# A decoder step on one core: another order of the mixers' work for the scheduler, with the retention projections 1.6 times further apart

## The chip, the cores and the metric

The kernel runs on one core of one Trainium2 chip. The metric is the device time of one execution in microseconds, as the median of several runs. The engines are TensorE (PE in the profile; PEld is its weight loading), VectorE (DVE), ScalarE (ACT), GpSimd (POOL) and SyncE (SP), whose queue issues most of the DMAs.

## The reference

One inference step of a two-layer decoder over 512 prompt rows and 64 sample rows, 576 together, 1024 wide. Layer 0 has two mixers side by side: RWKV-7 time mixing (mixer A, 8 heads of 64) and retention (mixer B, 8 heads of 64). One input projection feeds both, and one output projection takes both. Cut to the core:

```python
def ab_mixer(x, ...):
    proj = x @ w_in
    pa, pb = proj[..., :A_PROJ], proj[..., A_PROJ:]
    ya, shift1, wkv1 = rwkv7_mixer(pa, ...)     # S = S*w + sa*(kk*a) + v*k, o = S r, step by step
    q, kr, vr, gate = jnp.split(pb, 4, axis=-1)
    ob, ret1 = retention(rope(q), rope(kr), vr, ret0, log_gamma)
    yb = silu(gate) * head_norm(ob, gn_g, gn_b)
    return concatenate([ya, yb]) @ w_out, shift1, wkv1, ret1

for l in range(2):
    y = ab_mixer(x) if l % 2 == 0 else conv_mixer(x)
    x = layer_norm(ALPHA * x + y)
    x = layer_norm(ALPHA * x + squared_relu_mlp(x))
```

The states at the end of both mixers and of the convolution are outputs too.

## The kernel before

Everything is held transposed: a tile has 128 columns of the model on its partitions and the 576 rows along it, in two halves of 288 (`GN`). A weight is loaded in fp32 and cut into a high and a low part of type fp32r (ScalarE casts, VectorE or GpSimd subtracts), and each product is three matmuls (`mm3`, lines 152 to 154): high by high, high by low, low by high. A tile of a projection is 8 x 2 x 3 = 48 matmuls of 288 columns.

The mixers of layer 0 come first, up to some 497 us; the rest (the trunk: layer norms, MLPs, the convolution layer) follows and isn't touched. In the mixers the heads go in pairs, p = 0 to 3, for either mixer. `build` (from line 1346) writes them as twelve generators, which are numbered in the order of the call of `drive` in line 1493:

- 0, `projs`: 28 projection tiles in the order of `SEQ`. n = 0 to 2 are mixer A's k, r, v of pair 0, 3 to 5 of pair 1, 6 to 9 retention's q, k, v, gate of pair 0, 10 to 12 mixer A's of pair 2, 13 retention's q of pair 1, 14 to 16 mixer A's of pair 3, and 17 to 27 the eleven tiles left for retention pairs 1, 2 and 3. Most are spilled to DRAM (`spill`, `spillA`) through the one tile stg. At the end the pools of the projections are closed, the tiles x are loaded into the room that this gives (line 1427), and 'proj' is done.
- 1 `pres` and 2 `stages`: the preparation of mixer A's pairs, one after the other (`pre`, `stage`; L700 is the first matmul of a stage).
- 3 to 6, `back(p)`: `inverse` (L791 and L803), `scan` (L847 to L875), `ya`. The scan has a chain of seven steps: a matmul into the PSUM tile ch (L863), then an addition on VectorE (L865). Then come the products into the PSUM tile po.
- 7 `samples`, the sample rows' state.
- 8 `ret_fronts` (loads, rope, transposes), 9 `ret_backs((0, 2))`, 10 `ret_backs((1, 3))`: the retention (`ret_back`, `hnorm`). `ret_fronts` starts when the last stage is done, and waits for 'proj' before pairs 2 and 3. `ret_back` accumulates in ch for pairs 0 and 2, in po for pairs 1 and 3 (the tile is called rpo there).
- 11 `wout`: the output projection in three parts (`WP`, line 1342): tiles y0 to y2 when 'proj' and 'ya2' are done, y3 to y5 when 'ya3', 'ret0' and 'ret1' are, y6 when 'ret2' is. Its sums in PSUM are called wa; L1306 and L1307 cut its weights, L1336 and L1338 add to x. The last tile, y7, is multiplied at the start of the trunk.

ch, po and other tiles exist once, so who takes one first holds up the next. A generator yields a number (how long its step counts), a condition, or a lock that is taken (1, name) or given back (-1, name).

What sets the order: `drive` advances the generators one step at a time and gives each step a number, `tc.cur_priority`. The scheduler that lays out each engine's instructions takes the ready one of the lowest number. In the kernel before, steps and numbers are a table of 424 pairs (generator, number), `SCHEDULE`, which `drive` reads out:

```python
    base = tc.cur_priority
    for c, p in SCHEDULE:
        tc.cur_priority = base + p
        next(gens[c], None)
```

Conditions and locks that the generators yield have no effect there; the table stands for them. In it generator 0 goes from 100000 to 120421, by 735 a tile, and the largest number is 132485, of `wout`. The engines' queues are in order, so the layout is fixed when the program is built.

Of the kernel before, what the change touches and what calls it, by code (L numbers as in the profile page):

```python
# [1222 lines left out]
def post(o):  # L1223
# [9 lines left out]
            c(sh[1:][None]), c(wk(o['swkv'])), c(rt(o['sret'])), c(cv[1:][None]))  # L1233


SCHEDULE = (
# [33 lines left out]
)  # L1270


def drive(tc, *gens):

    base = tc.cur_priority
    for c, p in SCHEDULE:
        tc.cur_priority = base + p
        next(gens[c], None)
    tc.cur_priority = base + max(p for _, p in SCHEDULE) + 10000


CFG = {(n, g): dict(ds=() if n else tuple(range(8)), dq=() if n else tuple(range(8)), sv=(7,), qv=(7,), pg=(1, 2, 3, 4, 5, 6, 7), mulv=(0, 3, 6), affv=()) for n in range(4) for g in range(2)}
# [63 lines left out]
def build(tc, i, o, coff):  # L1346
    nc = tc.nc
    T = Trunk(tc, i['w'], ahead=2)
    with ExitStack() as es:
# [9 lines left out]
        with ExitStack() as s1:  # L1359
# [48 lines left out]
            def projs():  # L1408
                for n, (kind, p, j) in enumerate(SEQ):
                    if kind == 'A':  # L1410
                        M.proj_A(p, j, 2 + n)
                    elif kind == 'S':
                        M.spillA(p, j, 2 + n)
                    else:
                        M.spill(2 + n, 'qkvg'[j] + str(p))
                    yield
                nc.sync.dma_start(o['shift'], M.sho)
                sx.close()
                xp = pool('xp', 1, sr, side='right')
                T.x = [xp.tile([P, NT], F32, name=f'x{k}') for k in range(KT)]  # L1420
                yr = pool('yr', 1, sq, side='right')
                M.y[6:8] = [yr.tile([P, NT], F32, name=f'y{k}') for k in (6, 7)]
                W.y[6:8] = M.y[6:8]
                W.wq = pool('wq', 1, sq, side='right')
                W.acc = pool('wacc', 2, se, space=PSUM)
                for k in range(KT):
                    nc.gpsimd.dma_start(T.x[k], i['x'][:, k])
                M.done.append('proj')
# [282 lines left out]
```

## Time and profile before

| | us |
|---|---|
| median of 3 runs | 1575.98 |
| lowest and highest run | 1573.06, 1576.76 |
| profiled execution, its own time | 1570.47 |
| its span, first to last instruction | 1568.7 |
| PE busy in it | 1476.0 (94%) |
| mean granted clock of PE | 0.968 |

Busy times are those of the profiled execution, counted from the start of its span. A matmul counts as busy from its start to its modelled end, and matmuls overlap, so a stretch in which PE is busy throughout may hold more or fewer of them. The clock is a share of full speed.

### The profile page before, as it was taken

To read this page: it belongs to the slowest core of one execution; us is meant where nothing else is said; L and a number is where in the kernel's file an instruction comes from. 1 tells how busy PE (TensorE), PEld (TensorE's weight loads), DVE (VectorE), ACT (ScalarE), POOL (GpSimd) and SP (SyncE) were. 2 spreads that over 40 slices of the span, in tenths; PEclk is the share of its full clock that TensorE was granted. 3 is DMA by queue.
4 is the path that set the end of the run, shared out by engine and by line. 5 is a ranking of instruction groups with operands and counts; after the bars stand their busy time and mean duration, and the time that the engine had idled before them with its cause. 6 is when DMAs were issued, how large, how long until landed. Compare 5 with 4: busy or idle time off the path is not lost.

```text
span 1568.7 us, 29898 instructions
## 1 busy us (share of the span) xinstructions
PE 1476.0 (94%) x11760; PEld 1421.9 (91%) x11760; DVE 1077.6 (69%) x2038; ACT 639.8 (41%) x1345; POOL 564.0 (36%) x643
## 2 busy tenths in 40 slices
PE   6999999998997889999999998989998999999995
PEld 6999898987886689999999997889988999999995
DVE  4656766675756795664846779899799575574755
ACT  4444334332233553342624545434365244251533
POOL 2032213336443551211302377555564121121355
PEclk9999999999898889999999999999999999999998
DMA  5333234435223013231322411223402314132221
GB/s 171 96 96 91 86 101 130 139 92 168 82 64 120 0 43 121 81 122 57 106 81 68 135 42 56 74 74 115 129 1 81 97 66 135 54 121 68 83 66 61
DMA packets 71197, 140.04 MB, mean 89 GB/s; under 512 B 21744, under 2 KB 31200, under 8 KB 71056
## 3 DMA queue, kind: packets, MB, share of 16 engines
q1 hardware_dynamic: 68224, 129.69, 26.6%
q0 software_dynamic: 1536, 5.57, 1.1%
q10 hardware_dynamic: 1296, 2.86, 0.6%
q8 instruction: 92, 1.51, 0.4%
q14 instruction: 49, 0.40, 0.1%
HBM read 124.39 MB, written 13.70 MB: 88 GB/s over the span
## 4 chain that ended last, share of the span: by engine, by line
PE 77%; DVE 11%; DMA 4%; POOL 4%; issue 3%; ACT 1%; SPq 1%; DVEq 0%; ACTq 0%; POOLq 0%
PE acc L152 21%; PE acc L153 21%; PE acc L154 21%; DVE wl L78 2%; PE mx L803 2%; DMA raw<-in_w 1%; DVE u L309 1%; POOL x L255 1%; DVE hl L78 1%; PE mx L700 1%; PE wa L152 1%; PE mx L542 1%; PE pq L283 1%; PE ps L283 1%; PE wa L154 1%
## 5 line engine op out<-in xcount | busy, mean ns | idle before, releaser
L77 ACT CAST wh<-raw 128x512 fp32r<-128x512 f32 x440 | 252.7, 618 | 411.2 <-PE acc L153 269.7
L78 DVE TENSOR_TENSOR wl<-raw,wh 128x512 fp32r<-128x512 f32 x440 | 330.2, 782 | 42.2 <-ACT wh L77 34.9
L153 PE MATMUL acc<-hl,wh 128*128 128x288 f32 x1180 | 349.0, 297 | 7.1 <-DVE hl L78 7.1
L154 PE MATMUL acc<-hh,wl 128*128 128x288 f32 x1180 | 348.6, 297 | 0.0
L152 PE MATMUL acc<-hh,wh 128*128 128x288 f32 x1180 | 344.4, 297 | 2.3 <-DVE ta L205 1.8
L153 PEld LDWEIGHTS acc<-hl,wh 128*128 128x128 f32 x1180 | 222.9, 189 | 8.0 <-DVE hl L78 7.5
L152 PEld LDWEIGHTS acc<-hh,wh 128*128 128x128 f32 x1180 | 221.2, 189 | 3.2 <-DVE ta L205 2.0
L154 PEld LDWEIGHTS acc<-hh,wl 128*128 128x128 f32 x1180 | 223.0, 189 | 0.3
L152 PE MATMUL acc<-xh,wh 128*128 128x288 f32 x480 | 148.3, 310 | 13.4 <-ACT xh L1395 12.4
L123 POOL TENSOR_TENSOR s<-raw 128x512 f32<-128x512 f32 x37 | 56.0, 1515 | 272.4 <-DMA raw<-in_w 206.1
L153 PE MATMUL acc<-xl,wh 128*128 128x288 f32 x480 | 146.2, 305 | 0.0
L154 PE MATMUL acc<-xh,wl 128*128 128x288 f32 x480 | 146.0, 304 | 0.0
L152 PE MATMUL acc<-ht,wh 128*128 128x288 f32 x444 | 130.9, 296 | 1.7 <-ACT wh L77 1.3
L153 PE MATMUL acc<-lt,wh 128*128 128x288 f32 x444 | 130.7, 295 | 0.0
L154 PE MATMUL acc<-ht,wl 128*128 128x288 f32 x444 | 130.5, 295 | 0.0
L123 POOL TENSOR_TENSOR raw<-raw 128x512 f32<-128x512 f32 x37 | 54.6, 1475 | 157.0 <-DVE raw L123 106.6
L152 PEld LDWEIGHTS acc<-xh,wh 128*128 128x128 f32 x480 | 91.5, 191 | 16.7 <-ACT xh L1395 12.8
L153 PE MATMUL acc<-lo,wh 128*128 128x288 f32 x352 | 105.2, 299 | 0.0
L152 PE MATMUL acc<-ho,wh 128*128 128x288 f32 x352 | 104.9, 300 | 0.1
L154 PE MATMUL acc<-ho,wl 128*128 128x288 f32 x352 | 104.9, 299 | 0.0
L153 PEld LDWEIGHTS acc<-xl,wh 128*128 128x128 f32 x480 | 91.5, 191 | 2.6 <-DVE xl L1396 0.7
L154 PEld LDWEIGHTS acc<-xh,wl 128*128 128x128 f32 x480 | 91.6, 191 | 1.5 <-issue 0.2
(461 smaller groups left out, 3498.0 us busy)
## 6 DMA issues: line engine op xcount, KB each, us to landing
raw<-in_w SPq DMA_DIRECT2D x160, 512.0 KB, 3.9
raw<-in_w SPq DMA_DIRECT2D x60, 256.0 KB, 2.9
A<-stg SPq DMA_DIRECT2D x9, 288.0 KB, 2.4
x<-in_x POOLq DMA_DIRECT2D x8, 288.0 KB, 7.4
out_y<-x SPq DMA_DIRECT2D x16, 144.0 KB, 1.8
wr<-in_w SPq DMA_DIRECT2D x16, 128.0 KB, 2.3
wr<-in_w SPq DMA_DIRECT2D x32, 64.0 KB, 2.0
kr<-A SPq DMA_DIRECT2D x6, 288.0 KB, 2.7
```

Source lines behind the costliest of these rows:

```text
L77: a = self.nc.scalar.copy(hi[:, s], src[:, s])
L78: b = self.nc.vector.tensor_tensor(out=lo[:, s], in0=src[:, s], in1=hi[:, s].bitcast(F32), op=ALU.subtract)
L123: tt = lambda e, o, x, y, op: e.tensor_tensor(out=o, in0=x, in1=y, op=op)
L152: nc.tensor.matmul(acc, lhsT=hi, rhs=xh, start=first, stop=False)
L153: nc.tensor.matmul(acc, lhsT=hi, rhs=xl, start=False, stop=False)
L154: nc.tensor.matmul(acc, lhsT=lo, rhs=xh, start=False, stop=last)
L255: e.tensor_tensor(out=t, in0=t, in1=c, op=ALU.subtract)
L283: self.nc.tensor.matmul(st[k], lhsT=self.ones1024, rhs=t, start=start, stop=stop)
L309: nc.vector.tensor_tensor(out=u, in0=r, in1=mn, op=ALU.subtract)
L542: self.nc.tensor.matmul(ps, lhsT=lhsT, rhs=rhs[:, o:o + n], start=True, stop=True)
L700: nc.tensor.matmul(both[h][:, i], lhsT=b3[q, c, h:h + 2].rearrange('p s t -> p (s t)'), rhs=la[q, c], start=True, stop=True)
L803: nc.tensor.matmul(ps[:, i], lhsT=bd(self.mb if n < 3 else self.Y0, j + i), rhs=v[:, j + i], start=True, stop=True)
```

## The change

The table goes. `drive` works its numbers out while the program is built: each generator has a clock of its own, a yielded number advances it by so many steps of `RATE`, a condition or a lock holds it until it is free, and the generator whose clock is lowest is advanced. `projs` yields 1 up to n = 15 and 1.6 from n = 16 on, so the eleven tiles from n = 17 on are 1176.6 apart instead of 735.4.

```diff
-SCHEDULE = (
-    (0, 100000), (1, 100000), (1, 100000), (2, 100000), (3, 100000), (4, 100000), (5, 100000), (6, 100000), (7, 100000), (8, 100000), (9, 100000), (10, 100000), (11, 100000),
...
-)
+RATE = (735.4, 69, 94, 102.8, 96.9, 129.4, 147, 133, 167.5, 137.3, 134, 148.1)
...
-    base = tc.cur_priority
-    for c, p in SCHEDULE:
-        tc.cur_priority = base + p
-        next(gens[c], None)
-    tc.cur_priority = base + max(p for _, p in SCHEDULE) + 10000
+
+    base, n = tc.cur_priority, len(gens)
+    time, wait, live, held, now = [100000.0] * n, [None] * n, set(range(n)), set(), 100000.0
+    def free(c):
+        w = wait[c]
+        return w is None or (w() if callable(w) else w not in held)
+    while live:
+        ok = [c for c in live if free(c)]
+        c = min(ok, key=lambda c: (max(time[c], now) if wait[c] is not None else time[c], c))
+        if wait[c] is not None:
+            time[c] = max(time[c], now)
+            if not callable(wait[c]): held.add(wait[c])
+            wait[c] = None
+        now = max(now, time[c])
+        tc.cur_priority = base + int(time[c])
+        try:
+            y = next(gens[c])
+        except StopIteration:
+            live.discard(c)
+            continue
+        if callable(y): wait[c] = y
+        elif isinstance(y, tuple):
+            if y[0] > 0: wait[c] = y[1]
+            else: held.discard(y[1])
+        else: time[c] += RATE[c] * (1 if y is None else y)
+    tc.cur_priority = base + int(max(time)) + 10000
...
-                    yield
+                    yield 1 if n < 16 else 1.6
```

## Rows read from the trace of the kernel before

**Rows 1.** The page: PE's busy tenths in 40 slices of the span.
```profile
PE   6999999998997889999999998989998999999995
```

**Rows 2.** Tile xh (count; ns min/median/max, first and last start): the projections' matmuls.
```profile
L152 PE MATMUL acc<-xh,wh x480: 288/295/609, 6.8 to 353.3; 128*128 128x288 f32 x160
```

**Rows 3.** Tile views of x and wa, same columns.
```profile
L1427 POOL DMA_DIRECT2D x<-in_x x8: 536/536/577, 354.1 to 357.9; - x8
L152 PE MATMUL wa<-hi,h x112: 288/296/609, 366.1 to 496.0; 128*128 128x288 f32 x112
L1338 DVE TENSOR_TENSOR x<-x,wa x32: 441/448/456, 449.3 to 497.0; 128x288 f32<-128x288 f32 x32
L246 PE MATMUL cps<-x,o x2: 684/766/847, 497.5 to 498.1; 128*128 128x288 f32 x2
```

**Rows 4.** Busy time by stretch: PE, PEld, DVE, ACT, POOL; clock, DMA share, GB/s.
```profile
207.00:353.50 146.50, 143.78 (x1523) 131.66 (x1522) 97.32 (x238) 50.89 (x122) 48.43 (x61) 0.98 0.39 114
353.50:497.50 144.00, 124.54 (x1219) 111.25 (x1217) 91.96 (x233) 47.73 (x129) 66.22 (x98) 0.90 0.36 112
```

**Rows 5.** PE in order of time (start, duration), from 331 to 335 us.
```profile
331.44 0.44 PE L152 MATMUL acc<-xh,wh 128*128 128x288 f32 x1
...
332.64 0.41 PE L154 MATMUL acc<-xh,wl 128*128 128x288 f32 x1
...
333.02 0.29 PE L153 MATMUL acc<-xl,wh 128*128 128x288 f32 x1
...
334.49 0.30 PE L152 MATMUL acc<-xh,wh 128*128 128x288 f32 x1
```

**Rows 6.** Busy time by stretch of tile wa alone: PE, PEld, DVE.
```profile
353.50:497.50 144.00, 62.46 (x336) 51.44 (x336) 20.53 (x48) 0.90 0.36 112
```

**Rows 7.** PE's groups from 353.5 to 497.5 us: busy, mean ns, idle before.
```profile
L1129 PE MATMUL rpo<-rvt,sc 128*128 128x64 f32 x64 | 8.4, 277 | 0.0
L1160 PE MATMUL mx<-rvt,rkm 64*64 64x64 f32 x128 | 5.7, 253 | 2.7 <-ACT hd L972 2.7
L803 PE MATMUL mx<-vv,mb 128*128 128x128 f32 x32 | 5.5, 330 | 0.0
L1131 PE MATMUL rpo<-rS,e 128*128 128x128 f32 x24 | 5.4, 318 | 0.0
L1102 PE MATMUL mx<-e 64*128 64x128 f32 x48 | 5.1, 285 | 0.0
L1144 PE MATMUL mx<-e,rs 64*64 64x8 f32 x128 | 4.4, 200 | 0.5 <-DVE rss L1139 0.5
L803 PE MATMUL mx<-la,mb 128*128 128x128 f32 x16 | 2.2, 281 | 0.0
L803 PE MATMUL mx<-vv,Y 128*128 128x128 f32 x16 | 2.1, 275 | 0.0
L791 PE MATMUL mx<-lm,T 128*128 128x64 f32 x16 | 1.9, 275 | 0.0
```

**Rows 8.** DVE in order of time: the last two sums of wout's second part.
```profile
474.03 0.82 DVE L1338 TENSOR_TENSOR x<-x,wa 128x288 f32<-128x288 f32 x2 [0.72 <-PE wa L154]
```

**Rows 9.** The page's groups: casts and subtractions of weights (busy, mean ns, idle before).
```profile
L77 ACT CAST wh<-raw 128x512 fp32r<-128x512 f32 x440 | 252.7, 618 | 411.2 <-PE acc L153 269.7
L78 DVE TENSOR_TENSOR wl<-raw,wh 128x512 fp32r<-128x512 f32 x440 | 330.2, 782 | 42.2 <-ACT wh L77 34.9
```

**Rows 10.** Tile views of ch and rpo.
```profile
L863 PE MATMUL ch<-la x112: 218/267/366, 159.0 to 418.5; 64*64 64x64 f32 x112
L958 DVE TENSOR_REDUCE hv<-rpo x4: 676/692/693, 386.1 to 475.1; 128x8 f32<-128x512 f32 x4
```

**Rows 11.** Line 700 from 262 to 330 us: pair 3's stage.
```profile
L700 PE MATMUL mx<-la,b x36: 272/272/373, 274.0 to 309.0; 64*128 64x128 f32 x36
```

**Rows 12.** Waits from 350 to 500 us: in total, times, longest.
```profile
POOL l L1307 <- ACT h L1306: 24.1, 11, 4.2
ACT h L1306 <- PE wa L153: 18.5, 14, 4.2
```

32 rows, old and new, of the table SCHEDULE are left out of this document.

## The prediction

> **What bounds the kernel now.** I read the views in this order: the page's busy slices, the busy time by stretch, the one tile that marks the end of the projections, the groups of the stretch behind it, and last the waits. TensorE (PE) is busy nearly everywhere, and the slices dip only around a third of the span [rows 1]. Cut at the last projection matmul (353.3 us [rows 2]) and at the first matmul of the first layer norm (497.5 us, when the last output-projection sum has landed [rows 3]), the picture is clear [rows 4]: from 207 to 353.5 us PE is busy 143.78 of 146.5 us at a clock of 0.98, so the projections and the chains beside them are bound by PE. From 353.5 to 497.5 us, which I call the tail, it is busy 124.54 of 144 us at 0.90. There the projections are used up; what is left are the last half of pair 3's recurrence, the four retention pairs and the output projection (wout).
>
> How much room the tail has needs a second look, since its matmuls are long where they stand alone. A projection or wout matmul of 288 columns follows its neighbour by 0.24 us at the low one of the clock's two levels, 1.2 GHz, and by 0.1335 us at the full one (5 steps from 331.44 to 332.64 us, 11 from 333.02 to 334.49 [rows 5]). wout's 336 matmuls need 336 x 0.1335 = 44.9 us back to back; they keep PE busy 62.46 us [rows 6]. So the chains are busy 124.54 - 62.46 = 62.1 us, and at the tail's clock of 0.90 I take that as 55.9 us of full-clock work. Demand 100.8 us in 144 us: 70%, 43 us of room.
>
> The page itself puts PE's busy time down as 124.54 us, which leaves 19.5 us of room. The Trainium skill (Perfetto Trace Analysis, Identifying the Most-Contended Engine) says that matmul busy time is a poor measure of headroom and that the busy time of weight loads is a better one. The row has it: 111.25 us of 144, so 32.8 us [rows 4]. By matmul busy time no gain above 19.5 us could come out of the tail; by that rule the limit is 32.8 us. None of my terms uses the two limits.
>
> **The change part by part.** *The order.* The planner is ordinary code, and its rule can be worked through on paper for the twelve generators, from the yields, locks and conditions in the text; all positions here are less 100000. The eleven projections from n = 17 on stood at 12552 to 19685 in the table and stand at 12943 to 24709 now; the end of the projections goes from 20421 to 25886. But the diff does more than its name says. The table holds the recurrence chains of pairs 2 and 3 at half a step of what RATE gives (a yield of 10 in pair 2's inverse is 646 there, 1294 now), and has single gaps shifted (ret_back of pair 3 stands still from 26877 to 30712). All that goes. So pair 2's state chain on the PSUM tile ch goes from 17026 to 21878, pair 3's from 21144 to 26088, pair 2's end from 18642 to 26152. Retention pairs 0 and 1 stay (19090 to 24440 before, 19818 to 25145 after), pairs 2 and 3 go from 23226 to 32187 to 28398 to 33725, and wout from 20421 to 26152. Pair 3's stage, on which ret_fronts waits, is a little earlier (17696 to 17306) and has projections up to n = 20 ahead of it instead of 23.
>
> *What is removed and added on the engines:* nothing. Every matmul, cast and DMA stays; only numbers differ.
>
> *What moves ahead of the last projection.* In the table the last projection stood before most of pair 3's inverse and before both retention backs; now pair 3's inverse and pairs 0 and 1 stand before it. From the tail's groups [rows 7]: pair 3's inverse is L791 and the three forms of L803, 1.9 + 5.5 + 2.2 + 2.1 = 11.7 us. Half of L1129, L1160, L1131 and L1144 is pairs 0 and 1: (8.4 + 5.7 + 5.4 + 4.4) / 2 = 12.0 us, and a third of L1102, 1.7 us. Their transposes and small groups I estimate at a quarter of those 13.7 us, 3.4 us. Together 28.8 us busy, times 0.90 = 25.9 us at full clock. The stretch before has 146.5 - 143.8 = 2.7 us idle, which the projections can fill. The last projection would end at 353.5 + 25.9 - 2.7 = 376.7 us.
>
> *What is left for the tail:* 100.8 - 25.9 = 74.9 us of PE work. At the 70% that the tail reaches now it takes 107 us: the first layer norm at 483.7 instead of 497.5, **13.8 us** earlier. The trunk behind it (1071 us) has the same instructions and is carried over at nothing; it hides nothing, so no cover can be lost there.
>
> *The bounds of that.* At best wout alone paces the tail. Its x tiles can only be loaded when the projections' buffers are closed: the eight loads are issued from 354.1 us, and the first wout matmul is at 366.1 [rows 3], 12.6 us after the last projection. Beside few chains a three-tile part adds its 16 sums from 449.3 to 474.9 us, 25.5 us; two such parts, and 22.6 us from there to 497.5 [rows 3, 8], make 12.6 + 51 + 22.6 = 86.2 us: end at 463, 34.6 us earlier. At worst wout keeps the pace that it has now (below).
>
> *Other engines and queues.* A moved projection takes two weight casts of 0.62 us and two copies along on ScalarE, two subtractions of 0.78 us on VectorE [rows 9], and on SP's queue two weight loads and a spill, moved past the loads of ret_front and of wout. VectorE is busy 92 and ScalarE 48 us of the tail's 144, and the DMA engines 0.36 of it [rows 4]; five or six moved tiles add under 10 us to VectorE in a stretch with 50 idle. I cost this at nothing; the cover is that idle time. If it is gone, a weight pair that comes late holds PE by about one cast and one subtraction, 1.4 us a tile, 8 us for six.
>
> *What waits now.* The locks on ch and po turn round: before, pair 2's chain took ch ahead of retention 0; now retention 0 takes ch first, then pair 2, pair 3, retention 2, and retention 1 takes po ahead of pair 2. Behind pair 2 stands wout's first part, which needs ya2. The four chains on ch end at 418.5 us now, and the first retention lets go of its tile behind L958 at 386.1 [rows 10]. In the new order pair 2's end and the last projection stand within 1500 of each other, so I expect pair 2 through at about 377 us and cost the turn at nothing; the dear end is that ch is freed at 386.1 as now, 9.4 us behind 376.7, with pair 2's seven steps still to come. That needs the retention to start earlier than now, and it starts behind stage 3, whose first matmul is at 274.0 and whose last at 309.0 [rows 11]. PE is full in between, so projections fill that hole, and a hold there need not come out at the end.
>
> **The rivals.** *(a) Slower: wout pays for starting late.* wout's first matmul is at 366.1 and the trunk starts at 497.5: 131.4 us, in which its weight chain waits (POOL's low halves for ScalarE's casts 24.1 us, the casts for PE 18.5 us) [rows 12]. If that distance is set by this chain and by the retention pairs and not by the PE work that moves away, it stays, and it begins at 376.7 + 12.6 = 389.3: end at 520.7, 23.2 us later, 1599 us. It decides from a distance of 497.5 - 389.3 = 108 us: above, the change loses. For it: wout's waits are long and PE isn't full. Against: in the second part it went at 25.5 us for 16 sums, with two retention pairs beside it.
>
> *(b) No change: the order does not move the work.* The scheduler takes the lowest number among what is ready. Where a chain waits for its own results, the projections behind it are taken anyway, as early as before; then the last projection stays near 353.5, and the tail keeps its work: 1576 us. For it: on ch each matmul step (L863) is followed by one on VectorE (L865), and PE is free between them. Against: up to 353.5 us PE is full [rows 4], so a higher number does lose its place.
>
> *(c) All of the room:* the bound above, 34.6 us earlier, 1541 us. It is the far end of the forecast.
>
> **How the numbers follow.** The profiled execution took 1570.47 us, 1.8 us more than its span of 1568.7; the sum gives 1570.47 - 13.8 = 1556.7. The median of the runs, 1575.98, lies 5.5 us above that execution, so I predict 1575.98 - 13.8 = 1562 us. Chances: forecast with its far end (c) 0.46; no change (b) 0.16; slower (a) 0.38. The slower case is heavy because two steps lead to it: all of wout waits for the later end of the projections, and its first part for pair 2 behind retention 0 on ch, of which I have priced the second at nothing. The measurement of this kernel can tell some 0.3%, 4.7 us, from no change: faster means below 1571, slower above 1581. The forecast's own range is 1542 to 1570; for 8 in 10 I take 1546 to 1599, which holds (b) and (a) up to its price.
>
> **What the profile after would show.** The last matmul from xh at about 377 instead of 353; the first layer-norm matmul (L246) at about 484 instead of 497.5; the granted clock of the tail above 0.90, PE busy up to 377 as full as now. Rival (a): the first wout matmul near 389 or later and L246 beyond 500. Rival (b): the last matmul from xh before 360. The prediction is wrong if the last projection ends late because PE stood idle before it, with ch waiting for retention 0, or if the trunk's length of 1071 us changes.

## The result, and the profile after

The changed kernel takes 1589.47 us (median of 6 runs, 1584.89 to 1595.86) where the kernel before takes 1575.74 in the same comparison: 1.0092 times as long, 95% interval 1.0067 to 1.0117. The forecast was 1562 us; the time lies inside the range of 1546 to 1599 that was taken for 8 in 10, but on the side of rival (a). The profiled execution took 1588.54 us with a span of 1586.8, 18.1 us longer than before. The medians are only 13.7 us apart, since the profiled execution of before lay 5.3 us under its median and this one 0.9; the sums below account for the two profiles.

Where the diff drops the table, the line numbers behind `drive` fall by 13: L1427 is L1414, L1336 and L1338 are L1323 and L1325, L1306 and L1307 are L1293 and L1294. The page's slices of PE and of its granted clock in the profile after [rows 1]:

```profile
PE   6999999998987889999999998999998999999995
PEclk9999999989879989999999998999999999999998
```

Tile views of xh, x, wa and cps after [rows 2, 3] (count; ns min/median/max, first and last start in us):

```profile
L152 PE MATMUL acc<-xh,wh x480: 288/295/610, 6.6 to 386.2; 128*128 128x288 f32 x160
L1414 POOL DMA_DIRECT2D x<-in_x x8: 536/536/579, 387.2 to 391.0; - x8
L152 PE MATMUL wa<-hi,h x112: 288/297/609, 404.3 to 514.4; 128*128 128x288 f32 x112
L1323 DVE SCALAR_TENSOR_TENSOR x<-x,wa x16: 444/453/456, 422.1 to 451.2; 128x288 f32<-128x288 f32 x16
L1325 DVE TENSOR_TENSOR x<-x,wa x32: 447/454/456, 472.6 to 515.0; 128x288 f32<-128x288 f32 x32
L246 PE MATMUL cps<-x,o x16: 403/405/510, 515.6 to 1527.9; 128*128 128x288 f32 x16
```

The last projection moved from 353.3 to 386.2 us, 33 us. The tail behind it, up to the first layer-norm matmul L246, shrank from 144.2 to 129.4 us, only 14.8. So L246 begins at 515.6 instead of 497.5, 18.1 us later, and that is the whole difference between the profiles: the trunk takes 1586.8 - 515.6 = 1071.2 us, as before.

Busy time by stretch after, the same two stretches as in [rows 4] (length; busy PE, PEld, DVE, ACT, POOL; clock, DMA share, GB/s):

```profile
207.00:386.50 179.50, 172.87 (x1725) 157.35 (x1724) 112.79 (x277) 54.76 (x135) 60.21 (x78) 0.94 0.36 107
386.50:515.60 129.10, 106.45 (x1006) 92.38 (x1004) 75.35 (x200) 41.87 (x113) 51.87 (x83) 0.84 0.34 111
```

A sum over these two lines, which the prediction should have done, shows where the time went. Busy time times granted clock is work at full clock; the rest of a stretch is lost, to idleness or to the low clock.

| us at full clock | before | after |
|---|---|---|
| ahead of the last projection: work | 143.78 x 0.98 = 140.9 | 172.87 x 0.94 = 162.5 |
| lost there | 146.5 - 140.9 = 5.6 | 179.5 - 162.5 = 17.0 |
| in the tail: work | 124.54 x 0.90 = 112.1 | 106.45 x 0.84 = 89.4 |
| lost there | 144.0 - 112.1 = 31.9 | 129.1 - 89.4 = 39.7 |
| work in both | 253.0 | 251.9 |
| lost in both | 37.5 | 56.7 |

The work is about the same: some 22 us of it went ahead of the last projection, as the change meant. (A clock rounded to 0.01 leaves about 1 us open in each product. Summed over slices of 2 us, work is 252.7 before and 254.9 after, and lost time 37.8 and 53.7.) Nothing is won by that, for the moved work costs ahead what it saves behind. What changes the time is what is lost, and that grew by 16 to 19 us: 11 ahead, 5 to 8 in the tail.

The lost time has two parts. PE idle is 22.2 us before and 29.3 after (length minus busy time); the low clock takes 15.3 before and 27.4 after (busy time times what the clock lacks to 1). So more than half of the growth is counted as low clock. All runs together say the same more weakly: the mean granted clock is 0.963 over the six runs after and 0.968 over the 18 runs of before beside e10, which is some 7 us over a run. This divides the loss; it does not say what caused it.

### The profile page after: what moved, and what is told of

Its sections match the earlier page's. It is cut to its first block, busy times and chain, and to the rows that moved or that the text cites. A ratio compares the mean times of both kernels' runs of the same rounds, so it can differ in the third digit from the quotient of the medians.

```text
span 1586.8 us, 29928 instructions
## 1 busy us (share of the span) xinstructions
PE 1488.3 (94%) x11760; PEld 1430.8 (90%) x11760; DVE 1073.8 (68%) x2038; ACT 639.6 (40%) x1345; POOL 562.9 (35%) x643
## 4 chain that ended last, share of the span: by engine, by line
PE 72%; DVE 13%; DMA 5%; POOL 4%; issue 3%; ACT 2%; SPq 1%; DVEq 0%; ACTq 0%; POOLq 0%
PE acc L152 19%; PE acc L153 19%; PE acc L154 19%; DVE wl L78 3%; PE mx L803 2%; DMA raw<-in_w 2%; DMA wr<-in_w 2%; DVE u L309 1%; DVE hl L78 1%; PE mx L700 1%; PE wa L152 1%; POOL x L255 1%; PE mx L542 1%; PE wa L154 1%; PE wa L153 1%
## 6 DMA issues: line engine op xcount, KB each, us to landing
out_y<-x SPq DMA_DIRECT2D x16, 144.0 KB, 1.9
```

## Experiments

Three causes were open. The floor: wout's chain of weights (load, cast, subtraction) keeps the tail from shrinking with the work in it. The turn: pair 2 comes late behind retention on ch and po, and holds wout. The table: it is not the spacing but what the planner (the new `drive`) loses against the table. Every ratio is to the kernel before in the same comparison, with its 95% interval.

**The tail's floor.** `e7_after_wout_once` is the changed kernel, `e8_before_wout_once` the kernel before, both with one edit. It leaves out seven eighths of wout's weight loads, casts and subtractions in the parts: each part uses its first column block's weights for all eight blocks. The matmuls stay.

```diff
-                hi, lo = self.weights(m, ks[j], n)
+                if m == 0: h['w', j] = self.weights(m, ks[j], n)
+                hi, lo = h['w', j]
```

> The change, with the weights of wout's three parts loaded and cut for the first column block only and used for all eight: it leaves out seven eighths of wout's weight loads, casts and subtractions; all 336 wout matmuls and all else stay. Theory 'weight chain' (the distance from the first wout matmul to the first layer norm, 111.3 us in the change, is set by load, cast and subtraction of wout's weights): distance 90 us or less, L246 at 495 or earlier, about 1565 us. Theory 'mixer chains' (retention pairs 2 and 3 and pair 3's recurrence end last, at 474 us in the change, and y7 behind them): distance 103 us or more, L246 at 507 or later, 1580 us or more.

> The same edit in the kernel before: it leaves out seven eighths of wout's weight loads, casts and subtractions. Distance in the kernel before 131.4 us. Theory 'weight chain': 110 us or less, L246 at 477 or earlier, about 1555 us. Theory 'mixer chains': 122 us or more, since retention 3 ends at 482 us there.

e7 took 1571.66 us, 0.9996 (0.998 to 1.0013); e8 took 1557.57, 0.9909 (0.9891 to 0.9928). L246 and the two stretches of e7:

```profile
L246 PE MATMUL cps<-x,o x16: 403/405/511, 496.5 to 1509.9; 128*128 128x288 f32 x16
207.00:383.80 176.80, 168.61 (x1726) 153.94 (x1725) 112.75 (x278) 54.81 (x135) 60.81 (x78) 0.97 0.37 108
383.80:496.50 112.70, 100.19 (x1006) 89.07 (x1005) 75.36 (x199) 30.99 (x78) 32.55 (x48) 0.88 0.30 98
```

The distance from the first wout matmul to L246 is 94.8 us in e7 and 118.9 in e8, between the bounds of the two theories in both. Without the weight chain the tail of the changed kernel takes 112.7 us instead of 129.1, with nearly the same work in it (88.2 us for 89.4): the chain costs 16.4 us there, and 12.3 in the kernel before (its tail in e8 is 131.7 us instead of 144.0). The floor is real, but both kernels pay for it, and with the chain gone in both the change still loses. By the medians it loses as much: 1571.66 against 1557.57, 1.0088 times as long (about 1.0063 to 1.0113), where it is 1.0092 with the chain; the chain costs 0.96% after and 0.91% before. The spans of the profiles of e7 and e8 are 11.7 us apart instead of 18.1, so by them the chain is at most a third of the loss, some 6 us.

Which link is it? `e6_after_3bufs` and `e5_before_3bufs` give the cut weights h and l three buffers instead of two:

```diff
-... tag=f'w{c}', name=c, bufs=2) ...
+... tag=f'w{c}', name=c, bufs=3) ...
```

> The change, with three buffers instead of two for the cut weights of wout (h and l); nothing is left out. Theory 'weight chain': one block more can be cut while PE is held by others, 5 to 15 us faster than the change, 1575 to 1585. Theory 'mixer chains': within 4 us of the change.

> The kernel before with the same three buffers. Theory 'weight chain': 3 to 10 us faster than the kernel before. Theory 'mixer chains': within 4 us of it.

e6 took 1585.3 us, 1.0086 (1.0069 to 1.0103), e5 1573.5, 0.9993 (0.9981 to 1.0005): nothing. `e12_after_wr4` and `e9_before_wr4` give the loaded weights four buffers instead of two:

```diff
-        t = self.wq.tile([P, 2 * P], F32, tag='wr', name='wr', bufs=2)[:, 0:n * P]
+        t = self.wq.tile([P, 2 * P], F32, tag='wr', name='wr', bufs=4)[:, 0:n * P]
```

> The changed kernel with four load buffers instead of two for the output projection's weights. Theory 1, the load waits that the trace of the changed kernel shows ahead of the casts (22.8 us in 14 waits) are waits for a free load buffer: they mostly go, the distance from the first output-projection matmul to L246 falls from 111 us to 95 to 103 us, and the time to 1574 to 1582 us. Theory 2, they come from DMA bandwidth in that stretch or from the casts themselves: 1586 us, within 4 us.

> The kernel before with four load buffers instead of two for the output projection's weights, nothing else. Theory 1, the output projection's weights come late because a load waits for the buffer that an earlier block still holds until its cast and subtraction are done: the distance from the first output-projection matmul to L246 falls from 131 us by 5 to 15 us, and the time to 1560 to 1568 us. Theory 2, the loads are late for the rate at which the queues move them, or the cast and subtraction themselves are the floor: 1573 us, within 4 us.

e12 took 1575.99 us, 1.0027 (1.0008 to 1.0046), e9 1565.66, 0.9956 (0.994 to 0.9971): each faster than the kernel that it edits, by 0.65% and 0.44%. Between the two the change still costs 0.71%. ScalarE's waits from 380 to 517 us after, and then the same three in e12 (total, times, longest):

```profile
ACT h L1293 <- DMA wr<-in_w: 22.8, 14, 3.3
ACT h L1293 <- PE wa L153: 11.3, 7, 4.2
ACT kh L1293 <- DMA wr<-in_w: 6.3, 4, 2.2
```

```profile
ACT h L1293 <- PE wa L153: 25.4, 18, 4.1
ACT kh L1293 <- DMA wr<-in_w: 5.6, 6, 2.9
ACT h L1293 <- DMA wr<-in_w: 4.6, 3, 3.0
```

In the changed kernel the casts wait mostly for loads. With four load buffers they wait for PE to free h and l, and the tail is 118.3 us:

```profile
207.00:381.10 174.10, 167.88 (x1728) 152.92 (x1728) 113.63 (x278) 54.84 (x135) 61.20 (x78) 0.98 0.37 110
381.10:499.40 118.30, 102.36 (x1006) 89.78 (x1004) 76.49 (x199) 41.55 (x113) 53.46 (x83) 0.87 0.37 121
```

So two load buffers cost the changed tail 10.8 of the chain's 16.4 us. One place is the order of time between the first and second part: there `Wout.keep` loads y7's eight weights (kh) through the same two buffers. ScalarE, then PE, from the end of the first part (start, duration; in brackets the idle time before and its releaser):

```profile
450.67 0.72 ACT L1293 CAST kh<-wr 128x128 fp32r<-128x128 f32 x2 [2.16 <-DMA wr<-in_w]
453.98 0.49 ACT L1293 CAST kh<-wr 128x128 fp32r<-128x128 f32 x2
459.39 0.21 ACT L1145 COPY rot<-mx 128x64 f32<-128x64 f32 x1 [4.40 <-PE mx L1144]
461.46 0.30 ACT L1293 CAST kh<-wr 128x128 fp32r<-128x128 f32 x1 [1.86 <-DMA wr<-in_w]
464.33 0.63 ACT L1293 CAST kh<-wr 128x128 fp32r<-128x128 f32 x2 [2.08 <-DMA wr<-in_w]
467.66 0.40 ACT L1293 CAST h<-wr 128x256 fp32r<-128x256 f32 x1 [2.01 <-DMA wr<-in_w]
```

```profile
461.65 0.42 PE L944 MATMUL mx<-cst,rot 128*64 128x128 f32 x1
468.12 0.61 PE L152 MATMUL wa<-hi,h 128*128 128x288 f32 x1 [6.04 <-ACT h L1293]
```

Most of these casts are preceded by some 2 us of waiting for their loads, and in between ScalarE stands 4.4 us behind a retention copy (L1145) that waits for PE. PE's next matmul is the second part's first, so it idled 6.04 us until that part's first weights were cut. The Trainium skill (Perfetto Trace Analysis, Optimization Strategy) says that a gap that keeps repeating on the engine that should be saturated can mean too few buffers for the next tile. Here the gap repeats on ScalarE, which is not that engine, and the trace agrees in part: with four buffers the waits of the casts for loads of h fall from 22.8 to 4.6 us, those for kh only from 6.3 to 5.6.

The sums of wout in tile x show where the 10.8 us lie. Those after stand in the section on the result; here are the first part's before, then both lines of e12 and of e7:

```profile
L1336 DVE SCALAR_TENSOR_TENSOR x<-x,wa x16: 435/448/455, 385.3 to 437.6; 128x288 f32<-128x288 f32 x16
```

```profile
L1323 DVE SCALAR_TENSOR_TENSOR x<-x,wa x16: 442/453/454, 416.5 to 446.0; 128x288 f32<-128x288 f32 x16
L1325 DVE TENSOR_TENSOR x<-x,wa x32: 436/454/455, 463.0 to 498.9; 128x288 f32<-128x288 f32 x32
```

```profile
L1324 DVE SCALAR_TENSOR_TENSOR x<-x,wa x16: 435/453/456, 420.8 to 449.5; 128x288 f32<-128x288 f32 x16
L1326 DVE TENSOR_TENSOR x<-x,wa x32: 446/454/455, 458.2 to 496.0; 128x288 f32<-128x288 f32 x32
```

The first part itself doesn't show the floor after the change: its 16 sums take 29.1 us, 29.5 in e12 and 28.7 in e7 (52.3 before). From its last sum to the second part's first it is 21.4 us after, 17.0 in e12, 8.7 in e7, and 11.7 before (437.6 to 449.3 [rows 3]). From there to the last sum it is 42.4, 35.9, 37.8 and, before, 47.7 us. So of the 10.8 us, 4.4 lie between the two parts and 6.5 behind that, and the gap between the parts is where the change made wout's own path longer, by 9.7 us.

**The turn on ch and po.** `e4_pair2_first` is the changed kernel, with retention 0 and 1 asking for ch and po only when pair 2 has taken them (comments added):

```diff
+        self.done.append(f'ch{p}')          # scan, behind the tile ch
...
+        self.done.append(f'po{p}')          # scan, behind the tile po
...
+        if p < 2: yield lambda: ('ch2', 'po2')[p] in self.done
         yield 1, lk                         # ret_back
```

> The change as it is, RATE and spacing, with one edit: retention pair 0 asks for ch only when pair 2 has taken it, and retention pair 1 for po only when pair 2 has taken that. Only the turn on the two PSUM tiles is undone; pair 2's other steps keep their late numbers. Theory 'turn': 1570 to 1582 us, pair 2's chain on ch before retention 0's products, L246 at 490 to 505. Theory 'spacing': 1585 to 1595 us. If pair 2 is late for its numbers (its inverse stands at 14685 to 19473) and not for the lock, no change against the change: 1585 to 1595 too, with the chain on ch starting no earlier than 340 us.

It took 1586.78 us, 1.0094 (1.0072 to 1.0115), as the changed kernel. In that kernel pair 2's last multiplication, on which wout's first sums wait, is at 416.75 us, not at 377 as I had it; the second line is the same step in e4, where it is line 1023:

```profile
416.75 0.81 DVE L1021 TENSOR_TENSOR y<-mx,y 128x288 f32<-128x288 f32 x2
385.18 0.44 DVE L1023 TENSOR_TENSOR y<-mx,y 128x288 f32<-128x288 f32 x1
```

In e4 the first sum is still at 417.4 and L246 at 514.8 instead of 515.6. So the turn is not the cause at this spacing: 32 us of pair 2's lateness are worth 0.8 us. What else held the first sums until 417.4 was not tested.

**Charges and spacing.** On the planner I took the spacing back and halved the charges that the table has halved. [5] and [6] are the recurrence chains of pairs 2 and 3, [8] is the front half of retention, which the table also holds at half (a first step of 670 in the planner is 335 there; the prediction had missed that one).

Put together from the five edits:

```diff
-RATE = (735.4, 69, 94, 102.8, 96.9, 129.4, 147, 133, 167.5, ...)
+RATE = (735.4, 69, 94, 102.8, 96.9, 64.7, 73.5, 133, 167.5, ...)   # e2, e3
+RATE = (735.4, 69, 94, 102.8, 96.9, 64.7, 73.5, 133, 83.75, ...)   # e10, e11
...
-                    yield 1 if n < 16 else 1.6
+                    yield 1                          # e1, e3, e10
```

> The planner of the change with its RATE, but every projection yields 1: the spacing alone is undone. Theory 'turn' (pair 2 stands behind retention 0 on ch and behind retention 1 on po, so that wout's first part waits for ya2): the turn is still there, so 1583 to 1600 us, with the last matmul from xh back near 355 us, the first sum of wout (L1323) still at 410 us or later, and the first layer norm (L246) at 508 us or later. Theory 'spacing' (projections that end later push the reload of x and all of wout back): back to 1570 to 1580 us, L246 near 497. Theory 'shifts' (the single shifts of the table are what is lost): slower than 1580 like every planner run.

> The change with the RATE of pairs 2 and 3 (entries 5 and 6) halved to 64.7 and 73.5, as the table has them; the spacing of 1.6 stays. Pair 2 then stands ahead of retention 0 on ch (17338 against 20367) and of retention 1 on po again. Theory 'turn': 1565 to 1580 us, the last matmul from xh at 375 to 385 us, pair 2's end (last addition of ya2) before it, L246 at 485 to 500. Theory 'spacing': as slow as the change, 1585 to 1595, L246 at 510 or later, because wout still starts behind the later projections. Theory 'shifts': slower than 1580.

> The planner with the halved RATE of pairs 2 and 3 and every projection yielding 1: the table of the kernel before without its single shifts. Theories 'turn' and 'spacing': 1571 to 1581 us, within 5 us of the kernel before, L246 at 493 to 502. Theory 'shifts': 1583 to 1595 us.

> The planner again, with the charges of three of its generators halved, as the gaps of the written table have them: the spilling stages of pairs 2 and 3 (RATE[5], RATE[6]) and the front halves of retention (RATE[8]); every projection takes one step. It is the nearest that the planner comes to the order of before. Theory 1, the 0.47% that the planner lost with two charges halved and projections at one step came from retention's fronts being charged double: the time is that of before, 1573 us, within 5 us, and the last projection's matmul ends at 353 to 356 us. Theory 2, it came from the single shifts of the table (steps of some hundred moved by hand), which no rate reproduces: 1577 to 1583 us again, and the layer-norm matmul L246 begins at 500 us or later.

> The same three charges halved, and projections 16 to 27 taking 1.6 steps each: the wider spacing alone, on the order nearest to that of before. Theory 1, the wider spacing costs by itself where retention's fronts are charged as in the table, because the last projection ends later (365 to 370 us) and with it the first output projection: 4 to 10 us above the same planner at one step. Theory 2, the wider spacing is free or a gain there, and the loss of the whole change comes from the charges: within 3 us of the one-step run, or below it.

| charges | spacing 1 | spacing 1.6 |
|---|---|---|
| full | e1: 1604.74, 1.0216 (1.0194 to 1.0238) | after: 1589.47, 1.0092 (1.0067 to 1.0117) |
| [5], [6] halved | e3: 1579.28, 1.0047 (1.0032 to 1.0062) | e2: 1583.8, 1.0077 (1.0062 to 1.0093) |
| [5], [6], [8] halved | e10: 1592.26, 1.0123 (1.0107 to 1.014) | e11: 1589.73, 1.0103 (1.0087 to 1.012) |

The same spacing is a gain of about 1.2%, a loss of 0.3% and nothing that can be told. None of the three theories holds throughout: e1 is slower than the turn's 1583 to 1600 us, e2 lies between the turn's and the spacing's ranges, and e3 lies inside the range that those two gave it, but 0.47% above before instead of within 5 us; 'shifts' fits e1 and e2 and misses e3 (1583 to 1595). At full charges pair 2 does hold wout (e1; order of time of VectorE, and tile wa):

```profile
426.74 0.46 DVE L1021 TENSOR_TENSOR y<-mx,y 128x288 f32<-128x288 f32 x1 [0.50 <-PE mx L542]
L152 PE MATMUL wa<-hi,h x112: 289/296/610, 371.0 to 531.0; 128*128 128x288 f32 x112
```

There the projections end at 348.7 us, wout's first matmul is at 371.0, and the first sums wait for pair 2 until 432. With the wider spacing pair 2 is through 10 us earlier (416.75), and the first sums come 10 us earlier (422.1). e10 fits neither of its theories: halving retention's charge did not bring the time of before back, it cost 0.76%, some 12 us, against e3. In e10 and e11 the last projection is at 372.4 and 372.5 us and L246 at 517.5 and 517.4: 12 to 14 us more work than in e3 stand ahead of the last projection (table below) at either spacing. That the earlier retention fronts put it there is how I read it; no run shows it by itself.

**The spacing alone, in the table.** `e13_table_16` leaves the table as it was and adds to the numbers of generator 0 what 1.6 steps instead of 1 add from n = 17 on. The steps keep the table's sequence, so who takes ch, po and the buffers first is as before. `e14_table_16_wr4` is e13 with four load buffers.

```diff
-    base = tc.cur_priority
+    base, k = tc.cur_priority, -1
     for c, p in SCHEDULE:
+        if c == 0:
+            k += 1
+            p += int(0.6 * 735.4 * max(0, k - 16))
         tc.cur_priority = base + p
```

> The table of before, its entries in their order, with one thing changed: the numbers of the projections from n = 17 on, and of the projections' end, are spaced 1.6 times wider (0.6 x 735.4 more for each). No charge is doubled and no single shift is undone. Theory 1, the spacing itself costs: it moves TensorE work ahead of the last projection and makes none disappear, while the time lost to idleness and low clock grows ahead of it and does not shrink behind it. Last xh matmul 368 to 385 us, L246 at 502 to 515 us, time 1577 to 1591 us. Theory 2, the spacing alone is free or a gain, and the loss of the change comes from the table's charges that the planner doubles and its shifts that it undoes: 1560 to 1574 us.

> The same respaced table with four load buffers for the output projection's weights instead of two. Theory 1, what moves ahead comes back behind only one for one at best, even where the loads no longer hold the output projection: 1567 to 1578 us, slower than the table as it was with four buffers (1565.7 us). Theory 2, with the loads out of the way the forecast holds and the tail shrinks by more than the work that left it: 1550 to 1562 us.

e13 took 1580.07 us, 1.0043 (1.0026 to 1.006); e14 took 1567.65, 0.9964 (0.9951 to 0.9976), which can't be told from e9's 0.9956 (1.0008 times it, about 0.9988 to 1.0028). The stretches of e13, with its last xh matmul at 373.0 us and L246 at 503.7:

```profile
207.00:373.20 166.20, 161.10 (x1730) 147.70 (x1729) 109.00 (x265) 55.15 (x133) 54.73 (x69) 1.00 0.38 112
373.20:503.70 130.50, 112.15 (x1024) 97.80 (x1023) 88.77 (x215) 43.16 (x118) 60.51 (x92) 0.84 0.38 117
```

The part of the change that its name gives is a loss of 0.43%, about half of the whole. And it does here what I predicted up to the last projection: that ends at 373 (376.7 predicted), PE is full, and no more time is lost ahead of it than before (5.1 us, 5.6 before). It loses in the tail alone: 94.2 us of work in 130.5, so 36.3 lost instead of 31.9. With four load buffers the loss is gone, and still there is no gain: on the table it is the two load buffers that make the wider spacing lose. The other half, from 1.0043 to 1.0092, goes with the table's charges, its shifts and its sequence of steps, all of which the planner works out anew; I have not split it further, and since no setting of the charges that I tried gives the table's order back, which of its shifts matter stays open.

The sum of the first section for all the kernels, from their two stretches each (us at full clock; in the last column the lost time as PE idle + low clock):

| kernel | last xh | L246 | work ahead + in the tail | lost ahead + in the tail | idle + low clock |
|---|---|---|---|---|---|
| before | 353.3 | 497.5 | 140.9 + 112.1 = 253.0 | 5.6 + 31.9 = 37.5 | 22.2 + 15.3 |
| after | 386.2 | 515.6 | 162.5 + 89.4 = 251.9 | 17.0 + 39.7 = 56.7 | 29.3 + 27.4 |
| e1, full, 1 | 348.7 | 532.1 | 132.1 + 121.6 = 253.7 | 9.9 + 61.5 = 71.4 | 37.7 + 33.6 |
| e3, two halved, 1 | 358.2 | 503.5 | 140.7 + 111.7 = 252.4 | 10.7 + 33.4 = 44.1 | 30.0 + 14.1 |
| e2, two halved, 1.6 | 369.0 | 508.1 | 149.7 + 102.1 = 251.8 | 12.5 + 36.8 = 49.3 | 28.1 + 21.2 |
| e10, three halved, 1 | 372.4 | 517.5 | 154.6 + 104.4 = 259.0 | 11.0 + 40.5 = 51.5 | 23.7 + 27.7 |
| e11, three halved, 1.6 | 372.5 | 517.4 | 152.9 + 104.6 = 257.5 | 12.8 + 40.1 = 52.9 | 31.2 + 21.8 |
| e13, table, 1.6 | 373.0 | 503.7 | 161.1 + 94.2 = 255.3 | 5.1 + 36.3 = 41.4 | 23.4 + 17.9 |
| e9, before, 4 load buffers | 353.1 | 491.7 | 140.6 + 112.1 = 252.7 | 5.7 + 26.3 = 32.0 | 19.4 + 12.6 |
| e12, after, 4 load buffers | 380.9 | 499.4 | 164.5 + 89.1 = 253.6 | 9.6 + 29.2 = 38.8 | 22.2 + 16.7 |
| e8, before, weights once | 354.0 | 485.9 | 141.1 + 111.7 = 252.8 | 6.1 + 20.0 = 26.1 | 18.8 + 7.3 |
| e7, after, weights once | 383.6 | 496.5 | 163.6 + 88.2 = 251.8 | 13.2 + 24.5 = 37.7 | 20.7 + 17.1 |
| e4, after, pair 2 first | 383.2 | 514.8 | 167.2 + 94.0 = 261.2 | 9.2 + 37.4 = 46.6 | 28.0 + 18.7 |
| e5, before, 3 buffers for h and l | 353.2 | 494.7 | 140.7 + 113.4 = 254.1 | 5.7 + 27.9 = 33.6 | 23.7 + 10.0 |
| e6, after, 3 buffers for h and l | 387.4 | 518.6 | 165.3 + 88.8 = 254.1 | 15.3 + 42.2 = 57.5 | 33.7 + 23.8 |
| e14, table, 1.6, 4 load buffers | 374.7 | 500.1 | 161.0 + 92.8 = 253.8 | 6.9 + 32.4 = 39.3 | 21.2 + 18.0 |

The work in both stretches stays within 9.4 us while L246 moves by 46 and the loss by 45. But all these kernels hold the same matmuls, so those 9.4 us are what the sum leaves open, and e4 shows it: against the changed kernel it has 10.1 us less loss, most of it in low clock, and is no faster. Differences below some 10 us in these columns say nothing by themselves; the growth of 16 to 19 us by the change is above that, its parts hardly are. Of the pairs that differ in the spacing, only e1 and after lose clearly less with the wider one, where pair 2 had stood in the way; before and e13, e3 and e2, e10 and e11 differ by 1.4 to 5.2 us.

## Why the prediction was wrong

**The step that failed is the carried-over 70%.** I took the tail's 74.9 us of remaining work at the efficiency of before, 107 us. That supposes that lost time shrinks with the work: 43 to 32 us (with 100.8 us of work, wout's matmuls counted by their spacing; by busy time and clock it is 31.9 us that had to shrink). The tail took 129.4 us, and those 22.4 us are the larger part of the 31.9 by which L246 came later than forecast; the other 9.5 are the last projection's. By busy time and clock the loss in the tail did not shrink, it went from 31.9 to 39.7 us (in slices of 2 us from 32.1 to 37.2): PE idle from 19.5 to 22.7, low clock from 12.5 to 17.0.

Part of that loss belongs to the weight chain (16.4 us by e7, of which the two load buffers are 10.8 by e12), and the gap between wout's first two parts grew by 9.7 us. I read it so: a chain keeps its length when other work beside it goes and loses its cover instead, as in the 6.04 us of idle PE ahead of the second part. e14 bears it out for the spacing on the table, where four load buffers end the loss. For the whole change it isn't enough: with the chain gone in both kernels the tail loses 24.5 us after and 20.0 before, so there too the loss did not shrink with the work, and the change costs 0.88%. What holds that rest stays open.

**The moved work was about right, its price ahead of the last projection wasn't.** I had 25.9 us moving; 162.5 - 140.9 = 21.6 moved. I let 2.7 us of idle time be filled; instead idle time there rose to 6.6 us and the clock fell from 0.98 to 0.94. So the last projection came at 386.2 instead of 376.7. In e13, where the chains keep the table's order, it came at 373.0. The prediction's own sign for this, PE idle there with ch waiting for retention 0, is not what the trace has: 3.7 of the 6.6 us are one wait of L492 for VectorE's L1006, and 0.4 are on ch.

**wout's start.** I put its first matmul 12.6 us behind the last projection; it came 18.1 behind it (404.3). The distance from there to L246 was 111.3 us. Rival (a) decided from 108 us at a start of 389.3, and both were passed. (a) had the sign and named wout's chain, which costs time in both kernels. That its 23.2 us came near the 18.1 of the profiles is luck, because two errors met: the start came 15 us later than it said, and the distance, which it kept at 131.4, shrank by 20.

**What I had costed at nothing.** The turn on ch and po came out dearer than my dear end (pair 2 at 416.75 us, for an expected 377) and yet cost 0.8 us by e4. The table's charges and shifts were seen to go and put at nothing beyond that turn; with the table's sequence they are worth about half of the result (1.0043 to 1.0092). The tail's clock, which the forecast put above 0.90, was 0.84. The trunk at 1071 us, and PE's work as a whole, were right.

**The room by either measure was no sign of a gain.** The weight loads' busy time, which the Trainium skill (Perfetto Trace Analysis, Identifying the Most-Contended Engine) takes for headroom, left 32.8 us in the tail before; after, it leaves 129.1 - 92.38 = 36.7, matmul busy time 22.7 instead of 19.5. Room grew by either measure while the kernel got slower.

**Rival (b)** was refuted by the last xh at 386. Its premise, that a projection runs wherever a chain waits, fails at least once in the trace: between 275.49 and 284.73 us no projection matmul started, though PE stood idle for 3.7 us of that behind one waiting matmul (below). Whether a projection had its weights ready then is not shown.

## What to carry to other kernels

Before forecasting a gain from moving work between two stretches, write each stretch as work (busy time times granted clock) plus lost time. Moving work changes the end only by the change in lost time, so name the wait that each lost us belongs to and say why it would shrink. Keep in mind how far the work itself comes out equal on kernels with the same instructions (here within 9.4 us). The time that a load, cast, subtraction chain loses did not shrink here with the work beside it; a deeper load buffer for that chain (four instead of two, 0.44% on the kernel before) did more than any other order that was tried. And when a tuned table is replaced by a rule, measure the rule without the new idea first.

## What the runs showed of the hardware

The granted clock fell to its low level, 1.2 GHz of 2.4, in stretches where PE was busy throughout. Four stretches of the profile after (columns as above):

```profile
270.00:280.00 10.00, 6.27 (x97) 5.52 (x95) 8.82 (x12) 2.00 (x4) 6.80 (x7) 0.94 0.49 138
280.00:290.00 10.00, 10.00 (x73) 8.94 (x73) 3.84 (x9) 1.92 (x4) 2.45 (x5) 0.72 0.25 46
320.00:330.00 10.00, 8.99 (x102) 8.03 (x103) 9.14 (x17) 5.36 (x14) 3.31 (x7) 1.00 0.19 60
330.00:340.00 10.00, 10.00 (x74) 8.64 (x71) 2.38 (x6) 1.38 (x6) 5.38 (x7) 0.50 0.15 20
```

Both times PE had been idle in the 10 us before, 3.7 us (one wait of 3.7 us, of the matmul L492 for VectorE's L1006) and 1.0 us, and then ran 10 us full at 0.72 and at 0.50. In e13 the stretches from 270 to 290 and from 320 to 340 us had 1.9 and 2.0 us of idle time, and the clock stayed at 1.00:

```profile
270.00:280.00 10.00, 9.39 (x81) 8.77 (x79) 9.73 (x26) 2.53 (x6) 1.82 (x5) 1.00 0.65 186
280.00:290.00 10.00, 8.73 (x66) 8.39 (x66) 6.46 (x7) 1.55 (x4) 6.62 (x4) 1.00 0.55 190
320.00:330.00 10.00, 8.02 (x160) 6.88 (x160) 8.98 (x25) 4.18 (x11) 6.42 (x8) 1.00 0.55 172
330.00:340.00 10.00, 10.00 (x83) 9.47 (x84) 9.39 (x20) 4.82 (x13) 6.96 (x10) 1.00 0.21 54
```

So I could not tell from idle time alone where the clock falls. At half clock a full 10 us loses 5, and such patches make some two thirds of the 11.4 us that the change lost more ahead of the last projection: 172.87 x 0.06 = 10.4 us went to the low clock there, before 143.78 x 0.02 = 2.9. They also differ between kernels that share that stretch: e12, e7 and e6, whose edits are in wout alone, lost 9.6, 13.2 and 15.3 us in it instead of 17.0. So up to 7 of the 11.4 us are no fixed price of the order.
